# A hybrid decoder layer on one core: where the matmul operands lie in SBUF, modulo 512 bytes

## The chip, the cores and the metric

The kernel runs on one NeuronCore of a Trainium2 chip. The core has a matrix engine (TensorE, PE in the profile; its weight loads are listed apart as PEld), three engines for elementwise work (VectorE or DVE, ScalarE or ACT, GpSimd or POOL), a queue engine that issues DMAs (SyncE or SP), and 16 DMA engines. Data that the engines work on lie in SBUF, a memory of 128 partitions; matmul results go to PSUM. An address in SBUF is an offset within the partition, the same for all 128.

The metric is the time of one execution on the device in microseconds; less is better. The time before is the median of three runs. The profile shows another, single execution.

## The reference, cut to what matters

One decoder layer over 256 tokens of width 2048, in float32:

```python
mod = (silu(c) @ w_mod + b_mod).reshape(B, 6, D)          # sh1, sc1, g1, sh2, sc2, g2
h = rmsnorm(x, norm_mix) * (1.0 + sc1) + sh1
proj = h @ w_in                                            # 2048 -> 5660
y = concat(gla(...), gated_deltanet(...), pool(...), forgetting_attention(...)) @ w_out
x = x + g1 * y
h = rmsnorm(x, norm_ffn) * (1.0 + sc2) + sh2
gate = causal_dwconv(h @ w_gate, conv_w) + conv_b          # 2048 -> 5632
x = x + g2 * ((silu(gate) * (h @ w_up)) @ w_down)          # 5632 -> 2048
out = rmsnorm(x, norm_final)
```

The four large products (`w_in`, `w_out`, gate and up, `w_down`) are nearly all of the matmul work.

## The kernel before

**Products in three matmuls.** TensorE takes the large products in the type float32r. To keep float32's accuracy, both operands are split into a high and a low part: `split` (L114) copies the source to the high part on ScalarE (L115) and puts the rest into the low part on VectorE (L100, through `tt`). A product is then the sum of three matmuls, high by high, high by low and low by high, all added in PSUM through `mm` (L96, so that every matmul bears L97 in the profile). A matmul has two operands in SBUF: one is loaded into the array first (128 columns of 4 bytes, so 512 bytes per partition), the other is streamed through it (256 or 512 columns, 1024 or 2048 bytes).

**The weights.** `load_split` (L158) brings 512 KB of weights from HBM to a tile `wr` by one DMA on SP and splits it into `wh` and `wl`. The tiles come from the pool `wp`: five buffers of `wr`, three each of `wh` and `wl`, four of `wm` (the rows of `w_mod`), each 4096 bytes per partition.

**The activations.** `bigA` (16 x 512 x 4 bytes = 32768 bytes per partition) holds the high and low parts of the first h (`HL`), then of the mixers' output y (`Y2`), then of the second h (`H2`). `AH` and `AL` (44 x 256 x 4 = 45056 bytes each) hold the parts of the gated products, silu(gate) times up.

**The stages, in order.**
1. Start (to about 90 us): constants, x, the first rows of `w_mod`, the vectors, h.
2. Input projection (to about 250 us): `gdn` accumulates in six PSUM tiles `acc`, `pair` in tiles `ext`. `pair` loads the weights and streams h, or for two of its kinds loads h and streams the weights. 256 columns each.
3. Mixers (to about 475 us): matmuls of many small shapes (`gdt`, `oxt`), mixed with the rest of the input projection and with parts of the modulation vector (`bgt`).
4. Output projection (`project`, L950; to about 545 us): five column blocks of `w_out`, three of 512 and two of 256. Here y is loaded and the weights are streamed, PSUM tiles `ext` and `wot`.
5. Second norm, then gate and up (`proj`, L1026; about 550 to 1050 us): the weights are loaded, h is streamed, 256 columns, eleven rounds of 2 x 192 matmuls, PSUM tiles `fpt`.
6. Down projection (L1063; to about 1293 us): `AH` and `AL` are loaded, the weights are streamed, three column blocks of 512 (3 x 264 matmuls) and two of 256 (2 x 264), PSUM tiles `fpt` again. In its first two blocks VectorE also builds the last part of the modulation vector.
7. Last norm and the output.

**Where tiles lie.** Nobody writes addresses. A pool's tiles follow one another in the order in which they first appear, each padded to a multiple of 32 bytes per partition, and pools follow one another. In front come 16 KB of the DMA's and four constants (128 bytes). Then `keep`, in this order with bytes per partition: `ident` 512, `crow` 512, `ones` 512, `sel` 8, `V1` 512, `V2` 216, `V3` 528, `CB` 176, `cond` 64, `mhalf` 64, `s2` 64, `sh2` 64, `bigA` 32768, `bigC` 16384, `ga` 4096, `x1s` 40. Then `wp` with the weights. After it come the pools of a stage: `cp` and `sp` in the first half, `ap_` with `AH` and `AL` in the FFN. `padded_shape` gives a tile more room than its own shape takes.

`crow` holds c as 16 rows and is read once, by a transpose at the start (L309). `x1s` and `fs` take sums of squares, ten numbers per partition each, for the second and the last norm.

Of the kernel before, what the change touches and what calls it, by code (L numbers as in the profile page):

```python
# [8 lines left out]
F32 = mybir.dt.float32  # L9
# [7 lines left out]
P = 128  # L17
D = 2048
KT = D // P
T = 256  # L20
NT = T // P
# [25 lines left out]
NG = len(GROUPS)  # L47

TAKE = (16, 12, 11)

ORDER = "gpfd"

# [21 lines left out]
def trunk_kernel(ctx: ExitStack, tc: tile.TileContext, x, c, w_mod, b_mod, norm_mix, norm_ffn, w_in,  # L74
# [3 lines left out]
    nc = tc.nc  # L78
# [11 lines left out]
    keep = ctx.enter_context(tc.tile_pool(name="keep", bufs=1))  # L90
    wp = ctx.enter_context(tc.tile_pool(name="wp", bufs=3))

    def kt_(shape, name, dt=F32):
        return keep.tile(shape, dt, name=name, tag=name)

    def mm(o, l, r, start=True, stop=True):  # L96
        PE.matmul(o, lhsT=l, rhs=r, start=start, stop=stop, skip_group_check=True)  # L97

    def tt(o, a, b, op):
        V.tensor_tensor(out=o, in0=a, in1=b, op=op)  # L100
# [4 lines left out]
    def tsc(o, a, s1, s2, op0, op1=None):  # L105
        if op1 is None:
            V.tensor_scalar(out=o, in0=a, scalar1=s1, scalar2=None, op0=op0)
        else:
            V.tensor_scalar(out=o, in0=a, scalar1=s1, scalar2=s2, op0=op0, op1=op1)

    def act(o, a, f, **kw):
        S_.activation(o, a, f, **kw)  # L112

    def split(hi, lo, src):  # L114
        S_.copy(hi, src)  # L115
        tt(lo, src, hi.bitcast(F32), ALU.subtract)
# [4 lines left out]

    ident = kt_([P, P], "ident")
    nc.sync.dma_start(ident, cst[:, K_ID:K_ID + P])
    crow = kt_([KT, P], "crow")
    nc.sync.dma_start(crow, c[0].rearrange("(k p) -> k p", p=P))
    ones = kt_([P, P], "ones")
    V.memset(ones, 1.0)

# [10 lines left out]
    mhalf = kt_([P, 16], "mhalf")  # L139
    V.memset(mhalf, -0.5)  # L140
    s2 = kt_([P, KT], "s2")
    sh2 = kt_([P, KT], "sh2")

    bigA = lambda: keep.tile([P, KT, 2 * T], F32R, name="bigA", tag="bigA")
    bigC = lambda: keep.tile([P, KT * T], F32, name="bigC", tag="bigC")
# [12 lines left out]
    def load_split(view, k0, nk, c0, n):  # L158
        wr = load(view, k0, nk, c0, n)
        wh = wp.tile([P, 1024], F32R, name="wh", tag="wh", bufs=3).rearrange("p (k n) -> p k n", n=n)  # L160
        wl = wp.tile([P, 1024], F32R, name="wl", tag="wl", bufs=3).rearrange("p (k n) -> p k n", n=n)
        split(wh[:, 0:nk], wl[:, 0:nk], wr[:, 0:nk])
        return wh, wl
# [10 lines left out]
    def gemv(col0, done, pst=None, ready=lambda: True, bias=None):  # L174


        acc = pst() if pst else keep.tile([P, 1024], F32, name="ga", tag="ga")
        if bias is not None:
            G.memset(acc, 0.0)
            nc.sync.dma_start(acc[0:1], bias)  # L180
        for k in range(0, KT, 2):
            wms = []
            for kk in range(2):
                wms.append(wp.tile([P, 1024], F32, name="wm", tag="wm", bufs=4))
                last_wm[0] = nc.sync.dma_start(wms[kk], wm_v[:, k + kk, col0:col0 + 1024])
            for kk in range(2):
                wm = wms[kk]
                if not pst:
                    accumulate(acc, wm, k + kk, bias is None)
                    continue  # L190
                for c in range(2):
                    o = 64 * kk + 32 * c
                    mm(acc[o:o + 32], cond[:, k + kk:k + kk + 1].to_broadcast([P, 32]), wm[:, c * 512:c * 512 + 512],
                       start=k == 0, stop=k == KT - 2)
            if k == KT - 2:
                while not ready():
                    yield
                with tc.high_priority():
                    if pst:
                        gr = wp.tile([P, 1024], F32, name="wr", tag="wr", bufs=5)[:, 0:512]  # L200
                        S_.copy(gr, acc)
                        done([(gr, sel[:, c:c + 1]) for c in range(2)])
                    else:
                        done([(acc[:, c * 512:c * 512 + 512], ones) for c in range(2)])
            yield

    def to_row(dst, n0, pst):
        def f(parts):
            for j, (src, one) in enumerate(parts):
                b = pst()  # L210
                mm(b, one, src)
                S_.copy(dst[:, n0 + j * 512:n0 + j * 512 + 512], b)
        return f
# [14 lines left out]
    with ExitStack() as ph:  # L228
# [59 lines left out]
        with ExitStack() as st:  # L288
            sp = st.enter_context(tc.tile_pool(name="sp", bufs=1, reuse_waits="tile"))
            acp = st.enter_context(tc.tile_pool(name="acp", bufs=1, space=PSUM, reuse_waits="tile"))  # L290
            xt = sp.tile([P, NT, D], F32, name="xt")
            r1 = sp.tile([P, P], F32, name="r1")
            r2 = sp.tile([54, P], F32, name="r2")
            r3 = sp.tile([2 * NF, P], F32, name="r3")
# [175 lines left out]
            def extras(g):  # L470
                ps = range(len(pairs) - TAKE[g], len(pairs)) if g < NG - 1 else range(len(pairs))
                for p in ps:
                    yield from pair(p, done[p], g + 1)
                    done[p] = g + 1
# [472 lines left out]
        chunks = ((0, 512), (512, 512), (1024, 512), (1536, 256), (1792, 256))  # L947
# [26 lines left out]
        x1 = bigC().rearrange("p (t d) -> p t d", t=NT)  # L974
        for t in range(NT):
            nc.sync.dma_start(x1[:, t], x_v[:, t])
        x1s = kt_([P, NT, len(chunks)], "x1s")
        with tc.tile_pool(name="op", bufs=2, reuse_waits="tile") as op:
            for n, (c0, w) in enumerate(chunks):
                ns, gs = slice(c0, c0 + w), slice(c0 % 1024, c0 % 1024 + w)  # L980
# [11 lines left out]
    with ExitStack() as ph:  # L992
# [27 lines left out]
                stt(H2[:, k, T:], h, sh2[:, k:k + 1], H2[:, k, 0:T].bitcast(F32), ALU.add, ALU.subtract)  # L1020

        ap_ = ph.enter_context(tc.tile_pool(name="ap", bufs=1, reuse_waits="tile"))
        AH = ap_.tile([P, NF, T], F32R, name="AH")
        AL = ap_.tile([P, NF, T], F32R, name="AL")

# [15 lines left out]
        with tc.tile_pool(name="gp", bufs=2, reuse_waits="tile") as gp:  # L1041
            for n in range(NF // 4):
                gt = proj(wg_v, 512 * n)
                ut = proj(wu_v, 512 * n)
                for i in range(4):
# [7 lines left out]
                    tt(cv, ut[i], cv, ALU.mult)  # L1053
                    split(AH[:, f], AL[:, f], cv)

# [2 lines left out]
        held = [nc.sync.dma_start(nft, norm_final.partition_broadcast(P))]  # L1058
        with tc.tile_pool(name="op2", bufs=1, reuse_waits="tile") as op:
            chunks = ((0, 512), (512, 512), (1024, 512), (1536, 256), (1792, 256))  # L1060
            fs = op.tile([P, NT, len(chunks)], F32, name="fs")
            f1 = op.tile([P, 4], F32, name="f1")
            for n, (c0, w) in enumerate(chunks):  # L1063
                ns = slice(c0, c0 + w)
                if c0 % 1024 == 0:
                    g2 = gemv(5 * D + c0, to_row(g2t, c0, fpt), bias=b_mod[:, 5 * D + c0:5 * D + c0 + 1024])
                a = [fpt()[:, 0:w] for _ in range(NT)]
                nk = 1024 // w
                for g in range(NF // nk):
                    wh, wl = load_split(wd_v, nk * g, nk, c0, w)  # L1070
                    for kk in range(nk):
                        k = nk * g + kk
                        for t in range(NT):
                            ts = slice(t * P, t * P + P)
                            mm(a[t], AH[:, k, ts], wh[:, kk], start=k == 0, stop=False)
                            mm(a[t], AH[:, k, ts], wl[:, kk], start=False, stop=False)
                            mm(a[t], AL[:, k, ts], wh[:, kk], start=False, stop=k == NF - 1)
                    if g % 2 == 1:
                        with tc.issue_after(held[0].ins):
                            next(g2, None)  # L1080
                for t in range(NT):
                    m_ = op.tile([P, 512], F32, name="m2", tag="m2")[:, 0:w]
                    tt(m_, a[t], g2t[:, ns], ALU.mult)
                    tt(m_, x1[:, t, ns], m_, ALU.add)
                    act(a[t], m_, AF.Square, accum_out=fs[:, t, n:n + 1])
                    tt(x1[:, t, ns], m_, nft[:, ns], ALU.mult)
            V.tensor_reduce(out=f1[:, 0:2], in_=fs, axis=AX.X, op=ALU.add)
            tsc(f1[:, 2:4], f1[:, 0:2], 1.0 / D, EPS, ALU.mult, ALU.add)
            G.tensor_tensor(out=f1[:, 0:2], in0=f1[:, 2:4], in1=mhalf[:, 0:2], op=ALU.pow)
            ov = out[0].rearrange("(t p) d -> p t d", p=P)  # L1090
            for q_ in range(4):
                qs = slice(q_ * 512, q_ * 512 + 512)
                for t in range(NT):
                    if t == 0:
                        tsc(x1[:, t, qs], x1[:, t, qs], f1[:, t:t + 1], None, ALU.mult)
                    else:
                        act(x1[:, t, qs], x1[:, t, qs], AF.Copy, scale=f1[:, t:t + 1])
                nc.sync.dma_start(ov[:, :, qs], x1[:, :, qs])
# [29 lines left out]
```

## Time and profile before

| what | value |
|---|---|
| median of three runs | 1309.55 us (1309.2 to 1314.0) |
| the profiled execution, its own time | 1308.08 us |
| its span, first to last instruction | 1306.3 us |
| mean granted TensorE clock | 0.987 |
| DMA, whole span | 312.11 MB, mean 239 GB/s |

The span is cut into stages by windows of the trace. A window gives for each engine the busy time and the count of its instructions, then the granted clock, the DMA engines' busy share and GB/s. [...]

### The profile page before, as it was taken

How to read it: one execution, taken by the hardware profiler on the slowest of the kernel's cores; microseconds unless marked ns; L12 is line 12 of the kernel's file. 1: busy time of each engine (PE TensorE's matmuls, PEld its weight loads, DVE VectorE, ACT ScalarE, POOL GpSimd, SP SyncE). 2: the span in 40 equal slices, each digit the busy share in tenths (PEclk: the TensorE clock that was granted, in tenths of full speed). 3: DMA queues.
4: the chain of work that ended last, by engine and by line, in shares of the span. 5: the costliest groups of instructions: out<-in, count | busy, mean ns of one | idle time of the engine just before them, and what ended most of it. 6: DMA issues, size and time to landing. Idle time of an engine off the chain costs nothing.

```text
span 1306.3 us, 22959 instructions
## 1 busy us (share of the span) xinstructions
PE 1253.5 (96%) x9335; PEld 1160.9 (89%) x9335; DVE 867.5 (66%) x1113; ACT 612.3 (47%) x912; POOL 23.3 (2%) x31
## 2 busy tenths in 40 slices
PE   2799999999999999999999999999999999999996
PEld 1799999898876788999999999999999988888896
DVE  7679797989763497676556555655555587974543
ACT  3455344774354454554445444444544444443432
POOL 0200000010000100000000000000000000000000
PEclk8799999999999999999999999999999999999998
DMA  9999998796567987466666666666666699876662
GB/s 323 287 367 376 318 334 297 256 338 213 163 237 240 329 317 270 146 181 191 186 187 188 184 191 182 190 183 190 186 186 187 186 366 373 313 250 191 193 181 82
DMA packets 174241, 312.11 MB, mean 239 GB/s; under 512 B 16172, under 2 KB 65331, under 8 KB 173495
## 3 DMA queue, kind: packets, MB, share of 16 engines
q1 hardware_dynamic: 174135, 310.65, 73.1%
q8 instruction: 73, 1.20, 0.4%
q14 instruction: 33, 0.27, 0.1%
HBM read 308.51 MB, written 2.10 MB: 238 GB/s over the span
## 4 chain that ended last, share of the span: by engine, by line
PE 91%; DMA 5%; DVE 1%; ACT 1%; SPq 1%; issue 1%; POOLq 0%; ACTq 0%; DVEq 0%
PE fpt L97 57%; PE ext L97 14%; PE wot L97 5%; PE gdt L97 4%; PE acc L97 4%; PE bgt L97 3%; DMA wm<-in_w_mod_dram 3%; DMA wr<-in_w_in_dram 2%; PE oxt L97 2%; DVE ga L103 1%; DMA wsm<-in_w_in_dram 0%; ACT wh L115 0%; ACT xT L1011 0%; DVE wl L100 0%; PE oxt L873 0%
## 5 line engine op out<-in xcount | busy, mean ns | idle before, releaser
L100 DVE TENSOR_TENSOR wl<-wr,wh 128x1024 fp32r<-128x1024 f32 x384 | 469.3, 1223 | 317.6 <-ACT wh L115 315.7
L115 ACT CAST wh<-wr 128x1024 fp32r<-128x1024 f32 x384 | 403.9, 1052 | 543.0 <-PE fpt L97 350.5
L97 PE MATMUL fpt<-bigA,wh 128*128 128x256 f32 x2816 | 497.3, 281 | 1.5 <-ACT bigA L112 1.5
L97 PEld LDWEIGHTS fpt<-bigA,wh 128*128 128x128 f32 x2816 | 431.9, 190 | 1.9 <-ACT bigA L112 1.7
L97 PE MATMUL fpt<-bigA,wl 128*128 128x256 f32 x1408 | 394.3, 281 | 0.0
L97 PEld LDWEIGHTS fpt<-bigA,wl 128*128 128x128 f32 x1408 | 264.2, 188 | 0.0
L103 DVE SCALAR_TENSOR_TENSOR ga<-wm,cond,ga 128x1024 f32<-128x1024 f32 x139 | 177.8, 1279 | 10.7 <-DMA wm<-in_w_mod_dram 9.6
L97 PE MATMUL fpt<-wl,AH 128*128 128x512 f32 (+1 forms) x440 | 152.9, 348 | 0.0
L97 PE MATMUL fpt<-wh,AL 128*128 128x512 f32 (+1 forms) x440 | 152.5, 347 | 0.0
L97 PE MATMUL fpt<-wh,AH 128*128 128x512 f32 (+1 forms) x440 | 142.5, 348 | 0.0
L97 PE MATMUL ext<-bigA,wh 128*128 128x256 f32 x768 | 137.7, 281 | 0.0
L97 PEld LDWEIGHTS ext<-bigA,wh 128*128 128x128 f32 x768 | 117.5, 189 | 3.1 <-DVE dS L100 0.8
L97 PE MATMUL ext<-bigA,wl 128*128 128x256 f32 x384 | 107.5, 280 | 1.8 <-DVE wl L100 1.7
L97 PEld LDWEIGHTS fpt<-wh,AH 128*128 128x128 f32 x440 | 83.3, 189 | 10.8 <-ACT wh L115 0.2
L97 PEld LDWEIGHTS fpt<-wh,AL 128*128 128x128 f32 x440 | 83.3, 189 | 10.5 <-issue 0.2
L97 PEld LDWEIGHTS fpt<-wl,AH 128*128 128x128 f32 x440 | 83.3, 189 | 10.5 <-issue 0.2
L97 PEld LDWEIGHTS ext<-bigA,wl 128*128 128x128 f32 x384 | 72.2, 188 | 3.1 <-DVE wl L100 2.2
L97 PE MATMUL acc<-bigA,wh 128*128 128x256 f32 x384 | 69.8, 288 | 4.9 <-ACT bigA L115 3.0
L97 PE MATMUL ext<-wh,bigA 128*128 128x256 f32 (+1 forms) x320 | 67.7, 304 | 0.0
L97 PEld LDWEIGHTS acc<-bigA,wh 128*128 128x128 f32 x384 | 60.2, 197 | 5.2 <-ACT bigA L115 3.1
L97 PE MATMUL wot<-wh,bigA 128*128 128x512 f32 (+1 forms) x256 | 63.0, 337 | 0.0
L97 PEld LDWEIGHTS ext<-wh,bigA 128*128 128x128 f32 x320 | 51.6, 188 | 5.5 <-issue 1.4
(338 smaller groups left out, 1132.1 us busy)
## 6 DMA issues: line engine op xcount, KB each, us to landing
wm<-in_w_mod_dram SPq DMA_DIRECT2D x192, 512.0 KB, 6.1
wr<-in_w_in_dram SPq DMA_DIRECT2D x88, 512.0 KB, 9.6
wr<-in_ffn_w_gate_dram SPq DMA_DIRECT2D x88, 512.0 KB, 3.8
wr<-in_ffn_w_up_dram SPq DMA_DIRECT2D x88, 512.0 KB, 3.8
wr<-in_ffn_w_down_dram SPq DMA_DIRECT2D x88, 512.0 KB, 4.2
wr<-in_w_out_dram SPq DMA_DIRECT2D x32, 512.0 KB, 3.7
xt<-in_x_dram SPq DMA_DIRECT2D x2, 1024.0 KB, 7.3
bigC<-in_x_dram SPq DMA_DIRECT2D x2, 1024.0 KB, 9.5
```

The lines of the kernel that those rows point to most:

```text
L97: PE.matmul(o, lhsT=l, rhs=r, start=start, stop=stop, skip_group_check=True)
L100: V.tensor_tensor(out=o, in0=a, in1=b, op=op)
L103: V.scalar_tensor_tensor(out=o, in0=a, scalar=s, in1=b, op0=op0, op1=op1)
L115: S_.copy(hi, src)
```

## The change

In `keep`, `crow` goes away (it moves to the first stage's pool `sp`, and its load goes with it), `sh2` is given the room of 56 columns, and `x1s` the room of 2 x 32. In the FFN's pool `ap_`, `fs` is put in front of `AH` with the room of 2 x 32; before, it was in the last stage's small pool. No other line changes, and no instruction of TensorE, ScalarE or VectorE is added or taken away.

By the sizes above, with each start modulo 512:

| tiles | before | after |
|---|---|---|
| `bigA` (h, y) | 352 | 0 |
| `wr`, `wh`, `wl`, `wm` of `wp` | 416 | 256 |
| `AH`, `AL` | 416 | 0 |
| weights minus `bigA` | 64 | 256 |
| weights minus `AH`, `AL` | 0 | 256 |

```diff
@@ -48,6 +48,8 @@
 TAKE = (16, 12, 11)
 
+SHIFT = 256
+
 ORDER = "gpfd"
@@ -121,8 +123,6 @@
     nc.sync.dma_start(ident, cst[:, K_ID:K_ID + P])
-    crow = kt_([KT, P], "crow")
-    nc.sync.dma_start(crow, c[0].rearrange("(k p) -> k p", p=P))
     ones = kt_([P, P], "ones")
@@ -139,7 +139,7 @@
     s2 = kt_([P, KT], "s2")
-    sh2 = kt_([P, KT], "sh2")
+    sh2 = keep.tile([P, KT], F32, name="sh2", tag="sh2", padded_shape=[P, KT + 40])
@@ -289,6 +289,8 @@
             xt = sp.tile([P, NT, D], F32, name="xt")
+            crow = sp.tile([KT, P], F32, name="crow")
+            nc.sync.dma_start(crow, c[0].rearrange("(k p) -> k p", p=P))
             r1 = sp.tile([P, P], F32, name="r1")
@@ -974,7 +976,7 @@
-        x1s = kt_([P, NT, len(chunks)], "x1s")
+        x1s = keep.tile([P, NT, len(chunks)], F32, name="x1s", tag="x1s", padded_shape=[P, NT, SHIFT // 8])
@@ -1020,6 +1022,7 @@
         ap_ = ph.enter_context(tc.tile_pool(name="ap", bufs=1, reuse_waits="tile"))
+        fs = ap_.tile([P, NT, len(chunks)], F32, name="fs", padded_shape=[P, NT, (512 - SHIFT) // 8])
         AH = ap_.tile([P, NF, T], F32R, name="AH")
@@ -1058,7 +1061,6 @@
             chunks = ((0, 512), (512, 512), (1024, 512), (1536, 256), (1792, 256))
-            fs = op.tile([P, NT, len(chunks)], F32, name="fs")
             f1 = op.tile([P, 4], F32, name="f1")
```

## The prediction

> **What bounds the kernel now.** I read the page first: the busy times, the slices and the chain that ended last.
>
> ```profile
> span 1306.3 us, 22959 instructions
> PE 1253.5 (96%) x9335; PEld 1160.9 (89%) x9335; DVE 867.5 (66%) x1113; ACT 612.3 (47%) x912; POOL 23.3 (2%) x31
> PE   2799999999999999999999999999999999999996
> PEclk8799999999999999999999999999999999999998
> PE fpt L97 57%; PE ext L97 14%; PE wot L97 5%; PE gdt L97 4%; PE acc L97 4%; PE bgt L97 3%; DMA wm<-in_w_mod_dram 3%; DMA wr<-in_w_in_dram 2%; PE oxt L97 2%; DVE ga L103 1%; DMA wsm<-in_w_in_dram 0%; ACT wh L115 0%; ACT xT L1011 0%; DVE wl L100 0%; PE oxt L873 0%
> L97 PE MATMUL fpt<-bigA,wh 128*128 128x256 f32 x2816 | 497.3, 281 | 1.5 <-ACT bigA L112 1.5
> L97 PE MATMUL fpt<-bigA,wl 128*128 128x256 f32 x1408 | 394.3, 281 | 0.0
> ```
>
> TensorE is busy nearly everywhere at the full granted clock, and 57% of the chain is the FFN's matmuls (`fpt`), which wait for nothing. But a matmul's listed 281 ns overlaps its neighbours, so it says nothing of the rate. What counts is the distance from one start to the next. I took windows in which TensorE never pauses and counted matmuls (columns: length, busy and count, clock, DMA share, GB/s).
>
> ```profile
> 138.00:155.00 17.00, 17.00 (x152) 1.00 1.00 332
> 168.00:185.00 17.00, 17.00 (x147) 1.00 0.98 326
> 476.00:512.00 36.00, 36.00 (x157) 1.00 0.89 322
> 521.00:543.00 22.00, 22.00 (x189) 1.00 0.62 184
> 567.00:1046.00 479.00, 479.00 (x4069) 1.00 0.63 187
> 1060.00:1090.00 30.00, 30.00 (x134) 1.00 1.04 397
> 1231.00:1293.00 62.00, 62.00 (x519) 1.00 0.45 137
> ```
>
> A count includes the two or three matmuls that began before the window (281 ns over some 118 ns, 2.4 of them; 1.7 for 512 columns). So 256-column matmuls come every 17.00/149.6 = **113.6 ns** at 138 us (input projection), every 17.00/144.6 = **117.6 ns** at 168 us (the same stage), every 479.00/4066.6 = **117.8 ns** in gate and up, every 22.00/186.6 = 117.9 ns at the end of the output projection, and every 62.00/516.6 = **120.0 ns** in the last two column blocks of the down projection. The starts say the same; here are eight matmuls of the three rates:
>
> ```profile
> 137.22 0.39 PE L97 MATMUL ext<-bigA,wh 128*128 128x256 f32 x2
> ...
> 138.13 0.28 PE L97 MATMUL ext<-bigA,wl 128*128 128x256 f32 x1
> 699.77 0.28 PE L97 MATMUL fpt<-bigA,wh 128*128 128x256 f32 x1
> ...
> 700.71 0.28 PE L97 MATMUL fpt<-bigA,wh 128*128 128x256 f32 x1
> 1239.80 0.28 PE L97 MATMUL fpt<-wh,AH 128*128 128x256 f32 x1
> ...
> 1240.76 0.28 PE L97 MATMUL fpt<-wh,AL 128*128 128x256 f32 x1
> ```
>
> 0.91, 0.94 and 0.96 us for eight. So one form of matmul, at one clock and with no wait, runs at three rates. Each matmul has its own weight load, which runs beside the matmul before it. How fast can loads come? Where matmuls have one column only, the loads set the pace:
>
> ```profile
> 160.57 1.86 PEld L97 LDWEIGHTS ext<-ones,ga 128*128 128x128 f32 x16
> 162.36 0.30 PEld L97 LDWEIGHTS ext<-bigA,wh 128*128 128x128 f32 x2
> ```
>
> Sixteen loads in 162.36 - 160.57 = 1.79 us: 112 ns each. That is within 2 ns of the best matmul rate. Load and stream are nearly level, so anything that makes one of them stumble over the other shows at once in the spacing.
>
> **Where the operands lie.** The tiles' sizes, each rounded up to 32 bytes per partition, give the places. Before the change the weights' parts (`wh`, `wl`) begin 64 bytes past `bigA` modulo 512, since only `x1s` (40 bytes) stands between them with sizes that are no multiple of 512. `AH` and `AL` follow the weights' pool, so their distance to the weights is 0 modulo 512. Slices step by 512 or 1024 bytes, so that the distance holds for every matmul. By stage: distance 64 gives 113.6 or about 117.8 ns, distance 0 gives 120.0 ns. The pair at 521 and 1231 us is the cleanest, since the roles are the same there (activations loaded, weights streamed): 117.9 at 64, 120.0 at 0. Distance is thus one candidate for what separates the rates. It isn't the only one: the input projection shows 113.6 and 117.6 at the same addresses, and it changes from one to the other at a pause of TensorE and then keeps its rate. In gate and up the last such pause is at 567 us; from there it stays in the 117.8 state for all of 479 us.
>
> **The change part by part.**
>
> *The shift itself.* No instruction is added or removed on TensorE, ScalarE or VectorE. `sh2` is padded so that `bigA` (h, y, then h again) falls on a multiple of 512, `x1s` is padded to 256 bytes, which puts all parts of the weights 256 bytes off, and `fs` (256 bytes) in front of `AH` and `AL` brings these back to multiples of 512. The distance becomes 256 in all four projections, the farthest that 512 allows. No stage of the trace has this distance, so its rate is bounded by rows: 113.6 ns, the best seen, and 120.0, the worst. I take 113.6: from distance 0 to 64 the spacing falls by 2 ns and the unstretched state becomes possible at all, and 256 goes further the same way. It is an extrapolation over two points, and I give it no more than that.
>
> The sum, at 113.6 in place of what each stage has:
> - gate and up: 4069 x (117.8 - 113.6) = 17.1 us. TensorE alone sets the pace there (DMA 0.63), and nothing else is near: see below.
> - down projection, the two blocks of 256: 528 x (120.0 - 113.6) = 3.4 us. Its three blocks of 512 stand at 30.00/(134 - 1.7) = 226.8 ns, twice 113.4, so unstretched already: 0.
> - output projection, the blocks of 256: 192 x (117.9 - 113.6) = 0.8 us. Its 288 matmuls of 512 columns run at up to 36.00/155.3 = 231.8 ns, with two foreign matmuls in that window; against 226.8 it is at most 1.4 us, of which I take half, 0.7.
> - input projection, 90 to 250 us: by their starts, some 780 of its 1353 matmuls (row below) stand in stretches with the 117 to 118 spacing and some 480 in stretches near 113. At most 780 x 4.0 = 3.1 us. The DMA share is 0.94 there, so half may turn into waits for weights: 1.6.
>
> ```profile
> 90.00:250.00 160.00, 158.18 (x1353) 155.28 (x1353) 137.23 (x180) 81.27 (x114) 1.45 (x3) 1.00 0.94 315
> ```
>
> Together 17.1 + 3.4 + 0.8 + 0.7 + 1.6 = 23.6 us. Before 90 us and from 250 to 475 us (the mixers) I take nothing: there TensorE waits for DMAs or runs other forms.
>
> *What is late next.* In gate and up the other engines have room:
>
> ```profile
> 567.00:1046.00 479.00, 479.00 (x4069) 479.00 (x4068) 273.73 (x338) 227.39 (x297) 0.00 (x0) 1.00 0.63 187
> ```
>
> VectorE is busy 273.73 of 479.00 us (57%), ScalarE 227.39 (47%). At 479.00 - 17.1 us they stand at 59% and 49%. Only the weight load, at 112 ns, lies close behind.
>
> *The tiles that move.* `crow`'s load leaves the constants' block for the first stage's pool. It is still SP's second load, between `ident` and the loads of x; nothing is put ahead of it, and its 8 KB were issued here:
>
> ```profile
> L125 SPq DMA_DIRECT2D crow<-in_c_dram x1: 419/419/419, 1.2 to 1.2; - x1
> L1000 DVE TENSOR_REDUCE s<-x1s x1: 164/164/164, 545.7 to 545.7; 128x2 f32<-128x10 f32 x1
> ```
>
> Worst case, it slips behind one load: 0.4 us, and the queue before 90 us is full of weights that hide it. The reduce over `x1s` reads the same ten numbers with a wider step, 0.16 us; twice that would cost 0.2 us on the path. `fs` is only allocated earlier. I cost these at 0. The casts and subtracts of the weights move by 160 bytes with their tiles, as does what the DMAs write. Their price by alignment isn't in the trace; the only stretch that would show it is the first 90 us, where DMA is the bound, and 3% either way there is 2.7 us. I take 0 and keep it for the range.
>
> **The sum** against the profiled execution: its time is 1308.08 us, 1.8 more than its span. 1308.1 - 23.6 = 1284.5 us. The median of the runs is 1.5 above that execution, so the forecast is 1286 us, -1.8%. Its own range is 1279 to 1293.
>
> **The rivals.**
>
> *The addresses don't matter.* For it: 113.6 and 117.6 at the same addresses in one stage. The state seems chosen at a pause and kept. Then gate and up end in the same state as now and the time is 1309.5. Against it: the down projection holds 120.0 over some 520 matmuls, a rate that no stage at distance 64 holds. [...]
>
> *Only the low bits of the distance count.* If what matters repeats every 64, 128 or 256 bytes, then 256 is the same as 0, and every 256-column matmul locks at 120.0 as the down projection does. The place is gate and up first: 4069 x 2.2 = 9.0 us. The input projection adds 780 x 2.4 + 480 x 6.4 = 4.9 us (480 of its matmuls run near 113.6 now), the output projection 192 x 2.1 = 0.4; the mixers' share and the opening of gate and up some 2; the 512-column blocks of the output projection give 0.7 back. About +16 us: 1325. The point from which it decides is 118.3: above a spacing of that in gate and up nothing else pays for the loss. For it: 120.0 is the steadiest of the three rates. Against it: under a period of 64 the distances 0 and 64 would be the same already, and they are not.
>
> *It gains more.* All operands of float32r matmuls start 32 bytes off a multiple of 64 now, and at multiples of 64 afterwards. If the step of 113.6 itself comes from that, the load's 112 ns is the next bound: 4069 x 5.8 = 23.6, 528 x 8 = 4.2, 792 matmuls of 512 columns at up to 2 x 112 instead of 226.8 = 2.2 and as much again elsewhere, some 34 us: 1275; if the 512-column streams gain more, some 1265. No row shows any spacing below 113 for 256 columns. [...]
>
> *The change doesn't do what it says.* The padding could be rounded otherwise than I worked out, and the distance then isn't 256. It ends as one of the cases above; I give it no chance of its own.
>
> **How the numbers follow.** Forecast (113 to 115 ns in gate and up): 0.45. Part of it, 115 to 117: 0.07. More than it: 0.08. No change: 0.20. Slower: 0.20. So faster by over 0.5% (6.5 us, about what a measurement of this kernel can tell from no change) 0.60, the same 0.20, slower 0.20. The range goes from 1265 (more) to 1315 (no change and 0.4%, which takes in the alignment's 2.7 us); it leaves out the slower case, 2 in 10.
>
> **What would show it.** In the windows of the changed kernel: matmuls in 479 us of gate and up, 4069 now, about 4218 at 113.6, 3994 at 120.0; the last two down blocks, 519 in 62 us now, 548 at 113.6; the 512-column blocks unchanged at 134 in 30 us. If these blocks slow down while the 256 ones gain, the stream pays for the load. If gate and up stays at 117.8 and only the down blocks move, distance 0 was the only bad one, and the change is worth 3 us.

## The result and the profile after

The changed kernel takes 1322.62 us (median of 4, 1319.34 to 1323.75) against 1311.03 us before (median of 4, 1309.2 to 1314.0): ratio of the means 1.0082, 95% interval 1.0054 to 1.0110. It is slower, by about 0.8%. Forecast was 1286 us; the sign was wrong, and the time lies above the range of 1265 to 1315. One thing is needed to read the numbers below: the kernel before has two times of its own, near 1307 us in 63 of the 67 executions listed in this study (all four of the first comparison among them) and near 1287 us in the other four, and since the ratios on record leave out executions more than 1.5% above the fastest of their kernel, which here drops part of the long ones, means of all executions stand beside them.

The same windows as in the prediction, now of the changed kernel, moved where the stages moved (columns: length, TensorE busy and count, clock, DMA share, GB/s):

```profile
138.00:155.00 17.00, 17.00 (x144) 1.00 0.84 261
168.00:185.00 17.00, 17.00 (x144) 1.00 0.99 329
476.00:512.00 36.00, 36.00 (x161) 1.00 0.93 347
524.00:546.00 22.00, 22.00 (x185) 1.00 0.61 172
567.00:1046.00 479.00, 479.00 (x3994) 1.00 0.63 183
1090.00:1120.00 30.00, 30.00 (x133) 1.00 1.01 386
1246.00:1308.00 62.00, 62.00 (x519) 1.00 0.45 137
```

With 2.4 cut matmuls taken off as before, every window of 256 columns shows 120 ns to within one matmul of the count: 17.00/141.6 = 120.1 twice, 22.00/182.6 = 120.5, 479.00/3991.6 = 120.0, 62.00/516.6 = 120.0. Gate and up was at 117.8 and the input projection at 113.6 and 117.6; the end of the down projection was at 120.0 already and has the same count, 519 in 62 us. In gate and up the count is 3994, the number that the prediction gave for 120.0.

Where do the 14.8 us between the two spans (1306.3 and 1321.1) come from? The rows of the tile `fpt` give the first and the last start of gate and up, and of the down projection. Before:

```profile
L97 PE MATMUL fpt<-bigA,wh x2816: 276/281/385, 549.5 to 1046.7; 128*128 128x256 f32 x188
...
L97 PE MATMUL fpt<-wh,AL x440: 279/389/398, 1047.4 to 1293.3; 128*128 128x512 f32 x88, 128*128 128x256 f32 x59
```

After:

```profile
L99 PE MATMUL fpt<-bigA,wh x2816: 280/283/580, 553.6 to 1062.0; 128*128 128x256 f32 x188
...
L99 PE MATMUL fpt<-wh,AL x440: 279/389/396, 1062.7 to 1308.5; 128*128 128x512 f32 x88, 128*128 128x256 f32 x59
```

Gate and up takes 508.4 us in place of 497.2: **+11.2**. It also begins **4.1** us later; 3.4 of that stand already at the input projection's last `acc` matmul (243.5 against 240.1 us), the rest comes in the mixers. The down projection takes 245.8 us against 245.9, and what follows the last matmul 12.6 against 13.0: nearly nothing. The engines beside TensorE do the same work as before:

```profile
PE 1271.6 (96%) x9335; PEld 1180.2 (89%) x9335; DVE 868.5 (66%) x1113; ACT 611.2 (46%) x912; POOL 23.5 (2%) x31
PE fpt L99 57%; PE ext L99 17%; PE wot L99 5%; PE acc L99 5%; PE gdt L99 4%; PE bgt L99 3%; PE oxt L99 2%; DMA wm<-in_w_mod_dram 2%; DVE ga L105 1%; DMA wr<-in_w_in_dram 0%; ACT xT L1013 0%; SPq L401 0%; DVE wl L102 0%; SPq L400 0%; ACT wh L117 0%
```

VectorE's 868.5 us stand against 867.5, ScalarE's 611.2 against 612.3. What has changed is TensorE's spacing.

### The profile page after: what moved, and what is told of

Same layout as the page of the kernel before. It is cut to its first block, busy times and chain, and to the rows that moved or that the text cites. A ratio compares the mean times of both kernels' runs of the same rounds, so it can differ in the third digit from the quotient of the medians.

```text
span 1321.1 us, 22959 instructions
## 1 busy us (share of the span) xinstructions
PE 1271.6 (96%) x9335; PEld 1180.2 (89%) x9335; DVE 868.5 (66%) x1113; ACT 611.2 (46%) x912; POOL 23.5 (2%) x31
## 4 chain that ended last, share of the span: by engine, by line
PE 94%; DMA 3%; DVE 1%; ACT 1%; SPq 1%; issue 0%; POOLq 0%; ACTq 0%; DVEq 0%
PE fpt L99 57%; PE ext L99 17%; PE wot L99 5%; PE acc L99 5%; PE gdt L99 4%; PE bgt L99 3%; PE oxt L99 2%; DMA wm<-in_w_mod_dram 2%; DVE ga L105 1%; DMA wr<-in_w_in_dram 0%; ACT xT L1013 0%; SPq L401 0%; DVE wl L102 0%; SPq L400 0%; ACT wh L117 0%
## 5 line engine op out<-in xcount | busy, mean ns | idle before, releaser
L99 PE MATMUL fpt<-bigA,wh 128*128 128x256 f32 x2816 | 508.5, 284 | 1.5 <-ACT bigA L114 1.5
L99 PEld LDWEIGHTS fpt<-bigA,wh 128*128 128x128 f32 x2816 | 440.4, 192 | 1.9 <-ACT bigA L114 1.7
L99 PEld LDWEIGHTS fpt<-bigA,wl 128*128 128x128 f32 x1408 | 270.9, 192 | 0.0
L99 PE MATMUL ext<-bigA,wh 128*128 128x256 f32 x768 | 142.1, 285 | 0.0
L99 PEld LDWEIGHTS ext<-bigA,wh 128*128 128x128 f32 x768 | 120.1, 192 | 3.1 <-issue 0.8
```

## The experiments

### One size, nine values: the distance

The theories after the result. **Theory A**: what counts is the distance between the loaded and the streamed operand, and it repeats every 128 or 256 bytes, so that 256 is the same as 0. **Theory B**: what counts is where an operand begins modulo 64, which the change moved too (from 32 to 0). All kernels of this part are the changed kernel with another `SHIFT`, so that one distance holds in all four projections:

```diff
-SHIFT = 256
+SHIFT = 64        # 96, 128, 160, 192, 224; 32 and 512 with 512 bytes more room for x1s or fs
```

**d64**

> The changed kernel with SHIFT 64: bigA, AH and AL at multiples of 512, the weights 64 bytes past one, in every projection. Theory A (the distance counts, modulo 256 or 128): the 120.0 ns spacing goes away wherever it stands in the changed kernel; gate and up at 117.8 ns or 113.3, the last two down blocks at 117.8 or less instead of 120.0; time 1309 or less. Theory B (the start alignment counts: 32 bytes past a multiple of 64 was good, a multiple of 64 is bad): 120.0 ns everywhere, as with 256; time near 1322.

**d96**

> SHIFT 96: distance 96 everywhere, and the weights 32 bytes off a multiple of 64 while bigA and AH are on one. Theory A: not 120.0 ns; if the stretch falls with the distance up to half a period of 256, gate and up come nearer to 113.3 than at 64, time 1290 to 1309. Theory B (alignment of one operand): between the two, some 117 to 120. If 32 bytes count as well, a value of its own.

**d128**

> SHIFT 128: Theory A with period 128: 120.0 ns in every 256-column stage, as with 0 and 256, time near 1322. Theory A with period 256: 128 is the farthest point, so the smallest spacing, 113.3 ns in gate and up and in the last down blocks, time near 1286. Theory B: 120.0 ns, near 1322.

**d192**

> SHIFT 192: Theory A with period 128: the same as 64 (gate and up 117.8 or 113.3 ns). With period 256: 192 is 64 on the other side; 117.8 or 113.3 if only the size of the distance counts, another value if it also counts which operand is ahead. Theory B: 120.0 ns, near 1322.

**d32**

> SHIFT 32: distance 32 in every projection. Period 256, rate by distance: a value of its own, between 120.0 (distance 0) and the 117.8 or 113.3 of 64; by the mirror image of 96 (both 32 off a multiple of 64) some 118.7 to 120, time 1318 to 1322. If distances below 64 count as 0: 120.0 everywhere, 1322.

**d160**

> SHIFT 160, the mirror image of 96 about 128 (256 - 96). If only the size of the distance modulo 256 counts: 118.7 to 120 ns as at 96, 512-column blocks at 233, time near 1320. If the order of the operands counts: another value.

**d224**

> SHIFT 224, the mirror of 32 about 128. If only the size of the distance modulo 256 counts: gate and up at 118.3 ns, 512-column blocks at 233.3, near 1318. If the order counts, as between 96 and 160: another value, 118 to 120.

**d0**

> SHIFT 512 (fs with the room of 512 bytes): bigA, AH, AL and the weights all at multiples of 512, distance 0 everywhere. Period 256: the same as the changed kernel, 120.0 ns in every 256-column stage and 226.7 in the 512-column blocks, time near 1322. Period 512: gate and up at another value than 120.0.

And one kernel that keeps the distance of 256 but moves everything back by 160 bytes, to 32 past a multiple of 64:

```diff
-    sh2 = keep.tile([P, KT], F32, name="sh2", tag="sh2", padded_shape=[P, KT + 40])
+    sh2 = kt_([P, KT], "sh2")
```

**a256u**

> The changed kernel without sh2's padding: everything lies 160 bytes lower, so bigA, AH and AL begin 32 bytes off a multiple of 64 again, the distances stay at 256. Distance theory: 120.0 ns in all 256-column stages, 1322. Theory that the start alignment counts: the 117.8 and 113.3 of before come back in gate and up, near 1309.

Measured, one execution each (1308.10 and 1307.23 in the fourth column are medians of 11 and 29 executions, the others single ones). The count is that of gate and up, 567 to 1046 us; the spacing is 479.00 over the count less 2.4. The two columns to its right are the down projection, from the distances of its starts.

| kernel | distance | us | before on the same chip | count | gate and up | down, 256 columns | down, 512 columns |
|---|---|---|---|---|---|---|---|
| d0 | 0 | 1325.02 | 1308.10 | 3994 | 120.0 | 120.0 | 226.7 |
| d32 | 32 | 1317.90 | 1307.75 | 4050 | 118.3 | 116.7 | 233.3 |
| d64 | 64 | 1306.24 | 1305.87 | 4069 | 117.8 | 113.3 | 230.3 |
| d96 | 96 | 1320.46 | 1305.87 | 4039 | 118.7 | 120.0 | 233.3 |
| d128 | 128 | 1320.11 | 1305.87 | 4039 | 118.7 | 118.7 | 232.4 |
| d160 | 160 | 1328.47 | 1307.75 | 3994 | 120.0 | 117.3 | 234.3 |
| d192 | 192 | 1313.52 | 1305.87 | 4069 | 117.8 | 113.3 | 233.3 |
| d224 | 224 | 1309.63 | 1307.23 | 4102 | 116.8 | 118.4 | 233.3 |
| a256u | 256, all 160 lower | 1322.01 | 1307.75 | 3994 | 120.0 | 120.0 | 226.8 |

d0 and the changed kernel agree to the count, and 128 differs from both: **the distance counts, and 256 is the same as 0**. A repeat after 256 bytes fits this; it was tested at 0 and 256 alone. a256u shows that the start alignment doesn't count: 32 past a multiple of 64, and still 120.0; from the other side d64 has multiples of 64 and keeps the 117.8 of before. Theory B falls. That only the size of the distance counts falls too: 96 and 160 differ (118.7 and 120.0), and so do 32 and 224 (118.3 and 116.8). The farthest point, 128, is no good place either; my expectation of 113.3 there was wrong, and the thought that 96 might come nearer to 113.3 than 64 fell with it.

The table says more if the distance is counted with its sign, as the loaded operand's address less the streamed one's. In gate and up that is the distance of the table; in the down projection, where the roles are exchanged, it is 256 less that. Then the two stages agree: 118.3 and 118.4 at 32 (d32 and d224), 120.0 twice at 160 (d160 and d96), 116.8 and 116.7 at 224 (d224 and d32). At 96 they don't quite (118.7 and 117.3, d96 and d160), and at 64 and 192 one stage shows 117.8 and the other 113.3. One execution shows one rate only, so a distance may have others that this table misses.

The last blocks of d64 show the best rate held to the end of a stage:

```profile
1233.00:1291.00 58.00, 58.00 (x514) 1.00 0.45 146
```

58.00/511.6 = 113.4 ns, where distance 0 has 120.0. Yet d64 gains nothing over the kernel before: its 528 matmuls there give 3.5 us, and its 792 matmuls of 512 columns lose 792 x 3.6 ns = 2.9. With 512 columns only distances 0 and 256 keep 226.7 ns. A load at 112 ns (sixteen loads in 1.79 us before the change) takes less than half of that, so a delayed load would have room; that the stream itself is delayed is my reading, and no trace shows it.

### Two states at one distance

Gate and up and the last down blocks of d64 have the same shapes and the same distance, but 117.8 and 113.3 ns. The input projection of the kernel before shows both, too, and changes mostly at pauses or at stretches of other shapes. One more observation pointed the way: where that stage turns from streaming the weights to loading them, one pair of neighbours is at distance 0 (both in `wh`), and right there, without a pause, a stretch at 117.8 ends and one at 113.3 begins (110.2 us in d64, 210.9 us in the kernel before). Not always: at the same turn at 108.8 us the kernel before stays at 117.8. So I put such a pair into gate and up of the kernel before, called a kick here. It writes an accumulator that the next matmul clears, so nothing else changes:

```diff
             for g in range(KT // 2):
                 wh, wl = load_split(view, 2 * g, 2, c0, 512)
+                if g == 0:
+                    mm(a[0][:, 0], wh[:, 0, 0:P], wh[:, 0, 0:T])
```

**kick_in_64** (the kernel before, distance 64)

> The kernel before with one more matmul at the start of each of the 22 calls for gate and up: a slice of wh is loaded and wh itself streamed (distance 0 modulo 512 for one pair), into the accumulator that the next matmul clears; the result is the same. Theory of two states at distance 64 that keep themselves, one of which a single pair at distance 0 ends: gate and up goes from 117.8 to 113.3 ns and stays, 4224 x 4.4 - 22 x 0.12 = 16 us less, near 1290. Rival (the state is set by the addresses or by other engines, not by the history): gate and up stays at 117.8 and the time grows by 2.6 us.

**kick_in_256** (the changed kernel)

> The changed kernel with the extra matmul at the start of each gate and up call. Its pair has distance 0 modulo 512, among neighbours at 256. Theory (at 0 and 256 there is one state only): gate and up stays at 120.0 ns, the time grows by 22 x 0.12 = 2.6 us to some 1325. Rival (256 has a good state as well, and the changed kernel only happened to start in the bad one): gate and up at 113.3, near 1295.

Gate and up from 572 to 1030 us, kick_in_64:

```profile
572.00:1030.00 458.00, 458.00 (x4039) 1.00 0.66 193
```

and kick_in_256:

```profile
572.00:1030.00 458.00, 458.00 (x3819) 1.00 0.63 183
```

458.00/4036.6 = 113.5 ns, kicks included, and 1292.24 us against 1307.75: 15.5 us less, near the 17.1 that the prediction had hoped for in this stage, but at distance 64. At 256 it stays at 458.00/3816.6 = 120.0 and 1328.88 us against 1308.10. So distance 64 has a good state that keeps itself, and the kick found none at 256. The one execution of kick_in_64 was a lucky one, as the next part shows. The two states aren't a matter of the clock: the mean granted clock is 0.984 for kick_in_64 and 0.985 for the kernel before beside it.

### How reliably a kick works

**kick3** (three kicks; the first edit below is against kick_in_64, and `kick` is true for the second gate and the first up call), **kick3b** (the same, and four down blocks of 512)

```diff
-                if g == 0:
+                if g == 0 and kick:
...
+                if n == 3 and j == 0:
+                    mm(a[0], wh[:, 0, 0:P], wh[:, 0])
```

```diff
-            chunks = ((0, 512), (512, 512), (1024, 512), (1536, 256), (1792, 256))
+            chunks = ((0, 512), (512, 512), (1024, 512), (1536, 512))
```

> The kernel before with the extra matmul three times only: in the output projection's first block of 256, in the first up call and in the second gate call. If the good state keeps itself without being renewed: gate and up at 113.3 from the first up call on, the output projection's blocks of 256 at 113.3, 18 to 19 us less than before, near 1289, and some 3 us less than with 22 of them. If it decays: gate and up falls back to 117.8 at some point.

> kick3 with four column blocks of 512 in the down projection, in place of three of 512 and two of 256: 264 matmuls at 226.7 instead of 528 at 120.0, 3.5 us less, less what the wider last block adds behind the last matmul (some 1 to 2 us). Near 1287 if the end costs under 2 us.

**kick8** (gate 1 to 4, up 0 to 3), **kick22t** (the kernel of kick_in_64, timed), **kick22b** (with the four blocks)

> Eight kicks, in the first four up calls and the second to fifth gate call; none in the output projection. Chance theory: more runs in the good state than with three (two of six), fewer than or as many as with 22; good runs at 1290 plus or minus 2, bad ones at 1309. If the kick has one fixed effect per run: the same split as with three.

> The kernel with a kick in each of the 22 calls again, timed in rounds. If a kick takes the bad state to the good one with some probability and leaves the good one alone, nearly every run ends in the good state early: all runs at 1290 to 1294, none near 1309. If a kick can also end the good state, or the state is chosen otherwise, some runs stay near 1310.

> 22 kicks and four column blocks of 512 in the down projection: 1 to 2 us less than kick22t, so 1289 to 1292 in nearly every run.

| kernel | executions below 1300 us | before, below 1300 us | median | before, median | ratio on record, 95% interval | ratio of the means of all executions |
|---|---|---|---|---|---|---|
| kick3 | 2 of 6 | 1 of 11 | 1308.64 | 1308.10 | 0.9912, 0.9711 to 1.0114 | 0.9973 |
| kick3b | 5 of 6 | 1 of 11 | 1289.10 | 1308.10 | 0.9907, 0.9818 to 0.9996 | 0.9888 |
| kick8 | 3 of 12 | 0 of 29 | 1307.18 | 1307.23 | 0.9963, 0.9929 to 0.9998 | 0.9972 |
| kick22t | 4 of 12 | 0 of 29 | 1310.10 | 1307.23 | 0.9972, 0.9935 to 1.0008 | 0.9982 |
| kick22b | 4 of 12 | 0 of 29 | 1308.05 | 1307.23 | 0.9968, 0.9934 to 1.0002 | 0.9965 |

The expectations fell: 22 kicks do no better than three. Each kernel has two times some 17 us apart and little between. In the two profiles with a kick in the output projection, kick3 and kick3b, the spacing behind it stays at 117.8 ns. kick3b's profile (1285.87 us) is no evidence for kicks at all: its spacing stands at 113.3 ns already before the first kick of gate and up. This time the profile of the 22 kicks is one of the long executions:

```profile
572.00:1030.00 458.00, 458.00 (x3891) 1.00 0.60 186
```

458.00/3888.6 = 117.8 ns, through twenty kicks. Twenty kicks in vain don't look like chance at each kick. In the 117.8 state the starts come in a rhythm of three, the three matmuls of one product: on average one distance of 118.3 ns and two of 117.3 to 117.7, and which of the three gets the long one differs by stretch. A kick at a fixed place of the product meets the rhythm at two places in turn. The last pair puts the kicks before the first, the second and the third matmul of a call's first product in turn (`kick` is 2 n modulo 3 for gate, 2 n + 1 modulo 3 for up):

```diff
+                        three = ((wh, xh), (wh, xl), (wl, xh))
+                        for i, (w, x_) in enumerate(three):
+                            if k == 0 and f == 0 and i == kick:
+                                mm(a[1][:, 0], wh[:, 0, 0:P], wh[:, 0, 0:T])
```

**kickp**, **kickpb** (with the four blocks)

> The kernel with one kick in each of the 22 calls, in turn before the first, second and third matmul of the first product (into the call's other accumulator, which is cleared later). Orbit theory: the 117.8 ns state repeats over three matmuls, its place against the product differs by execution, and a kick ends it at one place only; with all three places tried, every run is at 113.3 ns from the third or fourth kick on, 1290 to 1295 in nearly all runs. Chance or per-run theory: a split as before, a quarter to a third near 1291, the rest near 1309.

> kickp with four column blocks of 512 in the down projection: 1 to 3 us less than kickp in the same state; under the orbit theory 1288 to 1293 in nearly all runs.

kickp: 8 of 10 executions below 1300 us, median 1293.24 against 1307.40, ratio on record 0.9967 (0.9901 to 1.0032), of all means 0.9936. kickpb: 8 of 12, median 1291.19, ratio on record 0.9939 (0.9877 to 1.0001), of all means 0.9932. Together 16 of 22, against 8 of 24 for kick22t and kick22b, which ran on another chip; the kernel before came out short in 3 of 21 on the one chip and in none of 29 on the other, so these counts alone don't settle it. The profile of kickp shows two kicks (matmuls that read `wh` alone), one in vain and one that works:

```profile
568.54 0.28 PE L97 MATMUL fpt<-bigA,wh 128*128 128x256 f32 x1
568.66 0.28 PE L97 MATMUL fpt<-wh 128*128 128x256 f32 x1
568.78 0.75 PE L97 MATMUL fpt<-bigA,wh 128*128 128x256 f32 x5
...
594.10 0.40 PE L97 MATMUL fpt<-bigA,wh 128*128 128x256 f32 x2
594.34 0.28 PE L97 MATMUL fpt<-wh 128*128 128x256 f32 x1
594.46 0.28 PE L97 MATMUL fpt<-bigA,wl 128*128 128x256 f32 x1
```

The windows after each of them:

```profile
571.00:594.00 23.00, 23.00 (x198) 1.00 0.64 186
597.00:1030.00 433.00, 433.00 (x3819) 1.00 0.66 193
```

After the kick before a second matmul, at 568.66 us, the spacing is 23.00/195.6 = 117.6 ns; after the one before a third, at 594.34, it is 433.00/3816.6 = 113.5 and stays. The place counts, and the other traces say how. In the profiles of the kicked kernels at distance 64, 35 kicks of gate and up meet the 117.8 state after the stage's opening pauses. The mean distances of the 12 matmuls ahead of each kick tell where the long one stands. Number the three matmuls of a product in a circle. All five kicks that end the state (kick_in_64, kick3, kick22b, kickp, kickpb) are put before one matmul while the long distance follows the next one in the circle. In the 30 in vain (21 of kick22t, 8 of kick8, 1 of kickp) the long distance follows the matmul that the kick is put before, or the one just ahead of the kick, and the kick only moves it from the one to the other.

This fits the counts. If a stretch begins with the long distance at any of the three places alike, which is assumed, kicks at a fixed place reach a third of the executions (8 of 24). Kicks that move on by one place in each call reach two thirds (16 of 22): where the long distance follows the matmul just ahead of the kick, it moves on by one place as well, and the next kick meets it the same way. That every execution would come round was not met: 6 of 22 stayed long, though no such execution was profiled. By the same rule kicks before the first, the second and again the first matmul would reach all three; that was not run.

Over all executions kickp, kickpb and kick3b gain 0.6 to 1.1%. By the ratios on record the gain isn't certain for kickp and kickpb, whose intervals contain 1. Which version is best these runs don't say: kick3b has the lowest mean, from six executions on a third chip. The four blocks of 512 are worth some 2.6 us: the short executions of kickpb average 1290.4 us, those of kickp 1293.1.

## Why the prediction was wrong

**What bounds the kernel**: right. TensorE's spacing in the float32r matmuls carried nearly the whole difference, the other engines' work stayed the same, and the change exchanged the rates of the windows for one another: 113.6 and 117.8 became 120.0.

**"From distance 0 to 64 the spacing falls by 2 ns ... and 256 goes further the same way"**: this step failed. Two points, 0 and 64, were taken for a slope in a quantity that is the same at 0 and 256. The runs put in its place a table in which 256 is the same as 0 and so has the worst rate of the kernel before, now in all stages. The forecast took 113.6 for gate and up where 120.0 came: 4069 x 6.4 ns = 26 of the 36.6 us of the error lie in this one term, and the same step is behind most of the rest (3.4 us not gained in the down projection, 1.5 in the output projection, 1.6 not gained and 4.1 lost up to the start of gate and up). The prediction called the step an extrapolation over two points, yet 0.45 of its chances stood on it.

**The rival that happened** is "only the low bits of the distance count". It gave 120.0 everywhere, 3994 matmuls in 479 us and 1325 us; measured are 120.0, 3994 and 1322.6. Its terms: gate and up 9.0 plus a part of "some 2", measured 11.2 (9.9 by the spacing, since the first 17 us of that stage had stood near 113 before, and 1.3 in short pauses at its start); the input projection 4.9, measured 4.1 with the mixers; the output projection about 0, as measured (68.2 us between its first and last `wot` start, before and after). Its chance, 0.20, was too small: the period was free, and a period of 128 or 256 bytes was as open as the one of 512 that the forecast needed without saying so.

**The argument against that rival** ("under a period of 64 the distances 0 and 64 would be the same already") was right, but it rules out 64 alone, and I used it against 128 and 256 as well.

**"It isn't the only one"**: the other half of the evidence was read and then not used. At distance 64 the input projection was in one state or the other for long stretches (it changed mostly at pauses or at stretches of other shapes, at 210.9 us at neither). So 113.6 was never the rate of a distance; it is one of two states seen at 64 (113.3 to 113.6 and 117.6 to 117.8 ns). By its time the kernel before ends in the good one in 4 of 67 executions; none of the four was profiled. No execution of the changed layout shows this state: gate and up stands at 120.0 in its profile, and under the kicks of kick_in_256. It is therefore slower twice over, by 12 to 15 us against the usual execution before, and by some 35 against the rare one.

**The rival "the addresses don't matter"** falls with the table: in the last down blocks the spacing differs by 6.7 ns (113.3 in d64, 120.0 in d0) with the operands' addresses alone. Which of load and stream waits, and on what, no trace shows.

**"It gains more"**: moving operands from 32 past a multiple of 64 onto one changed nothing (a256u against the changed kernel, d64 against before); no spacing under 113.3 was held for 256 columns, and none under 226.7 for 512.

**The costs at nothing** (`crow`, `x1s`, `fs`, the casts, the DMAs) were nothing that these runs can tell: a256u moves `bigA` and all tiles after it by 160 bytes and differs from the changed kernel by 0.6 us, and d64, which has all the moves at the distance of before, differs from the kernel before by 0.4 us.

## What to carry to other kernels

Where weight load and stream are nearly level (here 112 and 113.3 ns), the distance between the two operands' addresses in SBUF moved this kernel by up to 1.7% (1306.24 us at 64, 1328.47 at 160, one execution each), and it changes when a small tile in front changes its size (here `x1s`, from 40 to 256 bytes); measure the spacing by counting starts in a window without pauses, since the listed durations (281 against 283 ns) hide it. Don't draw a line through two addresses: here the effect came back to its start after 256 bytes (120.0 ns in gate and up at 0 and at 256), so sweep until it repeats before you believe in a slope. If one form of instruction shows two rates at the same addresses (here 113.5 and 117.8 ns in gate and up at distance 64), find out what switches between them before you give the better one to the change.

## What was not expected of the hardware

- At distances 64 and 192 a stream of 256-column matmuls has two rates, 113.3 and 117.8 ns, that can each last for thousands of matmuls (at 64: 4069 in one window of d64 at 117.8, 3819 in one of kickp at 113.5), and one matmul between, at the right place of the rhythm, can end the slower one (kickp at 594.34 us: 117.6 before it, 113.5 after). What the two states are inside TensorE was not found. In d192 gate and up stands at 117.8, the last down blocks at 113.3, and the input projection shows both.
- With 512 columns the order is turned round: 226.7 ns at distances 0 and 256, 230 to 234 at all others tried. The distance with the lowest spacing in gate and up, 64 (113.5 in kick_in_64), is a wrong one for the wide down blocks (230.3 in d64).
- Some of the rates lie one step apart: 113.3 and 120.0, 226.7 and 233.3 are 6.7 ns apart, and the three matmuls of the 117.8 state take 353.3, two such steps more than 3 x 113.3 = 340.0. The 118.7 of distances 96 and 128 doesn't fit (356.0, 2.4 steps), so this is no rule.
